# Low parts of the convolution module's weights made ahead and read back from DRAM, early products three pairs in turn, and one sum moved to the norms' PSUM banks, in a two-layer hybrid decoder trunk

## The chip, the cores and the metric

The kernel runs on one core of one Trainium2 chip. The metric is the device time of one execution in microseconds; several executions are timed and the median is given. One further execution was recorded by the hardware profiler, and the views below come from that one.

The engines are named as in the profile: PE is TensorE (matmuls), PEld its weight loads, DVE is VectorE, ACT is ScalarE, POOL is GpSimd, and SP is SyncE, which in this kernel issues every DMA from one in-order queue. L189 is line 189 of the kernel before.

## The reference

The sequence has 1024 positions of width 1024, everything in float32, and two layers. With `rms` for the RMS norm, the reference computes

```python
# layer 0
x = x + fox_attention(rms(x), ...)          # 16 heads, causal, with forget gates
u = rms(x) @ w_up[0]                        # (1024, 1024) @ (1024, 5632)
gate, val = split(causal_dwconv(u, 3 taps) + b, 2)
x = x + (silu(gate) * val) @ w_down[0]      # (1024, 2816) @ (2816, 1024)
# layer 1: the Conformer convolution module
a, g = split(rms(x) @ w_pw1 + b_pw1, 2)     # (1024, 1024) @ (1024, 2048)
u = causal_dwconv(a * sigmoid(g), 31 taps) + b_dw
x = x + silu(rms(u)) @ w_pw2 + b_pw2
# and a feed-forward block as in layer 0, with the weights of layer 1
```

## The kernel before, in words

**Split products.** TensorE reads operands in the type `float32r`. Each float32 operand is split into a high part, a cast (`hi`, on ACT, L183), and a low part, `raw - hi` (`lo`, on POOL or, with `vector=True`, on DVE, L184). `mm3` (L186) then issues three matmuls: high by high, high by low, low by high. So every 128x512 block of a weight costs one DMA, one ACT cast, one subtraction and twelve matmuls (or its share of them). The tiles rotate in rings: eight of `raw`, nine of `whi`, nine of `wlo`.

**Stages.** After the attention and its output projection come, for each layer, the up-projection, the down-projection, and, between the two feed-forward blocks, the convolution module. The sequence is worked in two halves of 512 positions. `trunk` (L973) writes the order of the work out by hand with Python generators: a generator yields after about one block of matmuls, `steps(gen, n)` advances one generator by n yields, and `turns(a, b, n, m)` alternates between two. From L1085 on PE's order is exactly the program's (`manual_schedule`). The order on the other engines and on SP's queue is laid out by the framework when the program is built, and on the chip each engine and SP's queue works strictly in that order.

**Up-projection.** The two halves of the sequence and the two halves of the width make a 2x2 block product that is computed with seven products in place of eight (`combine`, L243, makes the combined factors of the activations; `up`, L306, takes the 22 pairs of gate and value columns). A pair f needs four weight blocks and four sums of them on POOL (L334). Its seven products are called p1 to p7, twelve matmuls each, and their PSUM results are `x` (c11), `y` (c21), `z` (c12) and the sum `w` (c22), each a bank of the pool `pup`, which has six. PE's order within `up` is p1, p6, p2, p5 of pair f, then p4 and p3 of pair f-1, then p7 of pair f.

**Early products.** p1 and p2 need only the first half of the sequence, so `early` (L284) computes them ahead for some pairs, while the second half's norm and the factors are still being made. p1 goes to a PSUM bank and is copied by ACT (L294) to SBUF and from there to DRAM (`p1d`); p2 is then accumulated on the same bank, so its first matmul waits for that copy. The sum goes to DRAM too (`c11d`). In `up` such a pair (f < done) reads both back (L325, L326) and has five products in place of seven. Layer 0 has 12 such pairs, all made just ahead of `up`; layer 1 has all 22, made partly as filler inside the convolution module.

**Down-projection.** `down` (L221) accumulates four banks over 22 blocks of the gated activations, twelve matmuls a step. Per step it splits one block of activations (on DVE) and one of weights (on POOL). The first half of the sequence runs alone (L1109). The second half (`down1`) runs in turns with the convolution module's first half.

**Convolution module.** `conv` (L832) runs once per half. `glu` multiplies with `w_pw1` (48 matmuls for each of the eight column blocks, four weight blocks split on ACT and POOL). `taps_of` applies the 31 taps: 21 on DVE (L885), the other ten as ACT products (L889) summed by POOL (L890). The squares of all column blocks are summed by POOL (L899), and PE reads that sum (L916) before the norm. `rest` multiplies with `w_pw2`. The second half's filler is the first half's `rest` and then `early` of layer 1 (L1122).

**Norms and lag.** A norm block ends in eight PE transposes into the pool `pst` (two banks, also used by the DVE taps' accumulator). With `lag=True` they are put off by `LAG = 3` ticks; a tick is one yield of any generator, whether it held matmuls or not.

Of the kernel before, what the change touches and what calls it, by code (L numbers as in the profile page):

```python
# [16 lines left out]
P = 128  # L17
D = 1024
# [36 lines left out]
LAG = 3  # L55
LEAD = 11
# [12 lines left out]
class Trunk:  # L69
    def __init__(self, ctx, tc):  # L70
        self.tc = tc
        self.nc = tc.nc
        self.ctx = ctx
        self.cp = ctx.enter_context(tc.tile_pool(name="consts", bufs=1, reuse_waits="tile"))
        self.hp = ctx.enter_context(tc.tile_pool(name="ht", bufs=8, reuse_waits="tile"))
        self.mhalf = self.cp.tile([P, 32], F32, name="mhalf")
        self.ident = self.cp.tile([P, P], F32, name="ident")
        make_identity(self.nc, self.ident)
        self.nc.gpsimd.memset(self.mhalf, -0.5)
        self.uid = 0  # L80
        self.lagging = []

# [33 lines left out]
    def norm_block(self, scr, psum, tag, xt, out, tb, stag="scr", lag=False):  # L116
# [16 lines left out]
        if lag:  # L133
            self.lagging.append([LAG, lambda: [turn(q) for q in range(KT // 4)]])
        else:
            for q in range(KT // 4):
                turn(q)

    def tick(self):

        for w in self.lagging:
            w[0] -= 1
        if self.lagging and self.lagging[0][0] <= 0:
            self.lagging.pop(0)[1]()

    def flush(self):
        while self.lagging:
            self.lagging.pop(0)[1]()
# [37 lines left out]
    def mm3(self, out, lh, ll, rh, rl, start, stop, more=False):  # L186

        nc = self.nc
        nc.tensor.matmul(out, lh, rh, start=start, stop=False, skip_group_check=more)  # L189
        nc.tensor.matmul(out, lh, rl, start=False, stop=False, skip_group_check=more)  # L190
        nc.tensor.matmul(out, ll, rh, start=False, stop=stop, skip_group_check=more)  # L191

# [25 lines left out]
    def weight(self, src, shape):  # L218
        return self.halves(self.load(src, shape), shape)

    def down(self, xs, h, nh, lhs, rows, after=None):  # L221
# [4 lines left out]
        for j, (get, r) in enumerate(zip(lhs, rows)):  # L226
            hi, lo = get()
            wh, wl = self.weight(r[:, m], [P, 512])
# [55 lines left out]
    def early(self, l, ht0, w_up, p1d, c11d, count, half):  # L284
# [4 lines left out]
        for f in range(NF):  # L289
            a11, a12 = (self.load(wu[:, 4 * j : 4 * j + 4, f * P : (f + 1) * P], [P, 4, P]) for j in range(2))  # L290
            x = self.bank("e11")
            self.product(x, a11, b11h, b11l, True)
            t = self.ev("p1")
            nc.scalar.copy(t, x)  # L294
            nc.sync.dma_start(p1d[f], t)
            half[0] = True
            yield
            self.product(x, a12, b21h, b21l, False)
            t = self.ev("c11")
            nc.scalar.copy(t, x)  # L300
            nc.sync.dma_start(c11d[f], t)
            count[0] += 1
            half[0] = False
            yield

    def up(self, l, fac, w_up, tab, actd, done, p1d, c11d):  # L306
# [7 lines left out]
        def pair(f):  # L314
# [97 lines left out]
        for f in range(NF):  # L412
# [3 lines left out]
            before = c  # L416
            yield
# [3 lines left out]
    def down_acts(self, xs, l, h, actd, w_down, after):  # L421


        def get(f):
            return lambda: self.halves(self.load(actd[f][:, h * 512 : (h + 1) * 512], [P, 512]), [P, 512], True)

        rows = [w_down[l, f * P : (f + 1) * P, :] for f in range(NF)]
        for nh in range(2):
            yield from self.down(xs, h, nh, [get(f) for f in range(NF)], rows, after if nh == 1 else None)
# [402 lines left out]
    def conv(self, xs, xd, h, ht, w_pw1, taps, vec, w_pw2, halo, after, n_pool=N_POOL):  # L832
# [140 lines left out]
def trunk(ctx, tc, a):  # L973
# [69 lines left out]
    def begin(l, keep):  # L1043
        keep.update(
            done=[0], half=[False], p1d=[dram.tile([P, 512], F32, name=f"p1d{l}_{f}") for f in range(NF)],
# [3 lines left out]
    def early(l, keep):  # L1049
        yield from T.early(l, keep["ht0"], w_up, keep["p1d"], keep["c11d"], keep["done"], keep["half"])  # L1050
# [17 lines left out]
    def ffn_down(l, h, xd, after):  # L1068
        T.fetch_x(xs, xd, h)
        yield from T.down_acts(xs, l, h, actd, a["ffn_w_down"], after)  # L1070
# [14 lines left out]
    ctx.enter_context(tc.manual_schedule(engines={mybir.EngineType.PE}))  # L1085
    begin(0, keep)
# [3 lines left out]
    with ExitStack() as st:  # L1090
# [14 lines left out]
        def conv(h):  # L1105
            return T.conv(xs, xds[1], h, hc[h], a["conv_w_pw1"][0], taps, vec, a["conv_w_pw2"][0], halo,
# [3 lines left out]
        down1 = ffn_down(0, 1, xds[0], conv_norm)  # L1110
        steps(down1, LAG + 3)
        T.flush()
# [5 lines left out]
        steps(rest0, LAG + 4)  # L1118
        T.flush()
        main1, norm1, rest1 = conv(1)  # L1120

        def fill():  # L1122
            yield from rest0
            for _ in range(LAG + 1):
                yield
            T.flush()
# [35 lines left out]
```

## Time and profile before

| | |
|---|---|
| times of three runs | 2494.03, 2494.45 (median), 2496.71 us |
| the profiled execution's own time | 2495.49 us |
| its span, first to last instruction | 2493.6 us |
| PE busy | 2294.3 us (92%), 11282 matmuls |
| DVE, ACT, POOL busy | 1590.4, 1368.6, 1531.9 us |
| moved by DMA | 328.39 MB, mean 132 GB/s |

The profiled execution lies 1.04 us above the median, and its span 1.9 us below its own time. A busy PE is not PE at its peak: a 128x512 matmul is recorded with about 0.39 us, but the next one starts 0.23 us later, so back-to-back matmuls overlap in the records. What a stage of matmuls needs is read from the distance of their starts.

### The profile page before, as it was taken

Reading aid. Unit: us, or ns where it says so; the run is one execution under the profiler, and the core shown is the slowest. Engines: PE = TensorE matmul, PEld = TensorE weight load, DVE = VectorE, ACT = ScalarE, POOL = GpSimd, SP = SyncE. Lnnn points to the kernel's source line nnn. Section 1 sums busy time; section 2 is a strip of 40 time slices with the busy share of each in tenths; the row PEclk is TensorE's granted clock in tenths of the full one; section 3 lists DMA queues with packets and bytes.
Section 4 is the critical chain, followed back from the end, with each engine's and each line's share of the span. In section 5 each row is a group of like instructions: output and inputs, shape, how many; then the busy total and the mean of one; then the engine's idle time right before and its main releaser. Section 6 shows DMA issues by size and latency. Waiting matters only on the chain.

```text
span 2493.6 us, 34983 instructions
## 1 busy us (share of the span) xinstructions
PE 2294.3 (92%) x11282; PEld 1941.0 (78%) x11282; DVE 1590.4 (64%) x2769; ACT 1368.6 (55%) x2919; POOL 1531.9 (61%) x1322
## 2 busy tenths in 40 slices
PE   6899999999879999999999867969798999999999
PEld 6899999987757778888878756847576877778887
DVE  6577777774544675556569975878254676675554
ACT  6566666673444555555456555566453555554443
POOL 2354455451247877763479896879446878864443
PEclk9999999999989999999999988979899999999999
DMA  4222222342343442226554442325244444456664
GB/s 128 61 77 77 77 75 76 106 167 85 118 157 122 143 141 85 89 83 243 194 169 140 135 157 97 95 83 173 94 152 138 137 135 140 136 187 219 200 223 154
DMA packets 320856, 328.39 MB, mean 132 GB/s; under 512 B 22520, under 2 KB 227104, under 8 KB 320672
## 3 DMA queue, kind: packets, MB, share of 16 engines
q1 hardware_dynamic: 320672, 326.16, 40.9%
q8 instruction: 89, 1.46, 0.2%
q14 instruction: 95, 0.78, 0.1%
HBM read 253.13 MB, written 64.55 MB: 127 GB/s over the span
## 4 chain that ended last, share of the span: by engine, by line
PE 47%; POOL 8%; DVE 6%; issue 3%; ACT 3%; DMA 3%; SPq 0%; ACTq 0%; POOLq 0%; DVEq 0%
PE dn L189 7%; PE dn L190 7%; PE dn L191 7%; PE c L189 6%; PE c L190 6%; PE c L191 6%; POOL wlo L184 3%; POOL pacc L890 3%; DMA c<-c11d 2%; PE pw L189 2%; DVE acc L352 2%; PE pw L190 2%; PE pw L191 2%; PE e L189 2%; PE e L190 2%
## 5 line engine op out<-in xcount | busy, mean ns | idle before, releaser
L184 POOL TENSOR_TENSOR wlo<-raw,whi 128x512 fp32r<-128x512 f32 (+1 forms) x432 | 588.6, 1365 | 378.4 <-ACT whi L183 359.0
L183 ACT CAST whi<-raw 128x512 fp32r<-128x512 f32 (+2 forms) x612 | 367.7, 628 | 385.8 <-PE dn L190 212.4
L352 DVE SCALAR_TENSOR_TENSOR acc<-c,ffntab,acc 128x511 f32<-128x511 f32 (+1 forms) x352 | 266.9, 772 | 164.4 <-ACT acc L342 92.4
L189 PE MATMUL c<-bhi,whi 128*128 128x512 f32 x880 | 347.7, 395 | 22.8 <-DVE acc L352 19.2
L184 DVE TENSOR_TENSOR wlo<-raw,whi 128x512 fp32r<-128x512 f32 (+1 forms) x180 | 240.1, 1334 | 163.7 <-ACT whi L183 163.6
L191 PE MATMUL c<-bhi,wlo 128*128 128x512 f32 x880 | 342.9, 390 | 0.0
L190 PE MATMUL c<-blo,whi 128*128 128x512 f32 x880 | 342.8, 390 | 0.0
L184 POOL TENSOR_TENSOR wlo<-sum,whi 128x512 fp32r<-128x512 f32 x176 | 238.7, 1363 | 125.8 <-ACT whi L183 118.7
L189 PE MATMUL dn<-whi,whi 128*128 128x512 f32 x704 | 277.0, 394 | 7.2 <-DVE x L235 6.5
L191 PE MATMUL dn<-whi,wlo 128*128 128x512 f32 x704 | 275.4, 391 | 0.0
L190 PE MATMUL dn<-wlo,whi 128*128 128x512 f32 x704 | 275.4, 391 | 0.0
L885 DVE SCALAR_TENSOR_TENSOR cacc<-u,ctaps,cacc 128x512 f32<-128x512 f32 x320 | 237.1, 752 | 7.4
L189 PEld LDWEIGHTS c<-bhi,whi 128*128 128x128 f32 x880 | 165.1, 188 | 77.7 <-ACT acc L350 36.8
L342 ACT ACTIVATE acc<-c,ffntab 128x512 f32<-128x512 f32 x176 | 136.0, 788 | 132.6 <-DMA c<-c11d 124.1
L890 POOL TENSOR_TENSOR pacc<-pacc,prod 128x512 f32<-128x512 f32 x144 | 196.8, 1366 | 15.1 <-ACT prod L889 10.8
L191 PEld LDWEIGHTS c<-bhi,wlo 128*128 128x128 f32 x880 | 165.2, 188 | 35.2
L190 PEld LDWEIGHTS c<-blo,whi 128*128 128x128 f32 x880 | 165.3, 188 | 32.4
L189 PE MATMUL pj<-whi,hthi 128*128 128x384 f32 (+1 forms) x512 | 179.7, 352 | 6.7 <-ACT sqr L555 3.6
L113 POOL TENSOR_SCALAR ss<-ss 128x4 f32<-128x4 f32 (+1 forms) x96 | 22.5, 234 | 261.6 <-DVE ss L557 116.7
L190 PE MATMUL pj<-wlo,hthi 128*128 128x384 f32 (+1 forms) x512 | 177.4, 346 | 0.6 <-DVE wlo L184 0.6
L191 PE MATMUL pj<-whi,htlo 128*128 128x384 f32 (+1 forms) x512 | 177.8, 348 | 0.0
L643 POOL TENSOR_SCALAR x<-x,nm 128x896 f32<-128x896 f32 (+7 forms) x128 | 100.9, 793 | 104.6 <-DVE nm L642 72.5
(201 smaller groups left out, 5505.3 us busy)
## 6 DMA issues: line engine op xcount, KB each, us to landing
raw<-in_ffn_w_up_dram SPq DMA_DIRECT2D x244, 256.0 KB
raw<-actd SPq DMA_DIRECT2D x176, 256.0 KB
raw<-in_ffn_w_down_dram SPq DMA_DIRECT2D x176, 256.0 KB
raw<-in_conv_w_pw_dram SPq DMA_DIRECT2D x96, 256.0 KB
actd<-acc SPq DMA_DIRECT2D x88, 256.0 KB
raw<-in_fox_w_in_dram SPq DMA_DIRECT2D x64, 192.0 KB
xd<-x SPq DMA_DIRECT2D x24, 512.0 KB
x<-xd SPq DMA_DIRECT2D x24, 512.0 KB
```

Source lines behind the costliest of these rows:

```text
L113: nc.gpsimd.tensor_scalar(ss, ss, 1.0 / n, EPS, op0=ALU.mult, op1=ALU.add)
L183: self.nc.scalar.copy(hi, raw)
L184: (self.nc.vector if vector else self.nc.gpsimd).tensor_tensor(lo, raw, f32(hi), op=ALU.subtract)
L189: nc.tensor.matmul(out, lh, rh, start=start, stop=False, skip_group_check=more)
L190: nc.tensor.matmul(out, lh, rl, start=False, stop=False, skip_group_check=more)
L191: nc.tensor.matmul(out, ll, rh, start=False, stop=stop, skip_group_check=more)
L342: nc.scalar.activation(acc, ps, AF.Identity, bias=tap[3], scale=tap[2])
L352: nc.vector.scalar_tensor_tensor(acc[:, j:], ps[:, : 512 - j], tap[2 - j], acc[:, j:], op0=ALU.mult, op1=ALU.add)
L643: nc.gpsimd.tensor_scalar(X[:, :L], X[:, :L], nm[:, 2:3], 1.0, op0=ALU.mult, op1=ALU.mult)
L885: nc.vector.scalar_tensor_tensor(acc, win(j), tap(j), acc, op0=ALU.mult, op1=ALU.add)
L890: nc.gpsimd.tensor_tensor(pacc, pacc, t, op=ALU.add)
```

## The change

- **Early products three pairs in turn.** `early` runs p1 of three pairs before p2 of the first; from then on p1 and p2 alternate, two pairs apart. When `ffn_up` has used up the lead it sets `stop`, and `early` only finishes the open pairs. The lead in layer 0 falls from 11 to 8 pairs (`LEAD = (8, 11)`).
- **Low parts kept in DRAM.** During layer 0's `up`, 32 blocks of `w_pw1` and 44 of layer 0's `w_down` are loaded, cast on ACT, subtracted on DVE, and their low parts stored to DRAM (`split_ahead`): two after each pair with early products, four after each other pair, the rest after the last. Both halves of the convolution module and the second half of layer 0's down-projection (`down1`) then cast the high part on ACT as before and load the low part with a DMA. In `down1` the activations' low parts move from DVE to POOL (`los is None` becomes False).
- **One sum in the norms' banks.** `w` (c22) takes a bank of `pst` in place of one of `pup`.
- **Lag counted in matmuls.** The lagging transposes come 36 matmuls after their norm block, with at least 12 matmuls between blocks, in place of three ticks. Loops that ran a fixed number of steps now run until nothing is lagging.

The core of the diff:

```diff
-LAG = 3
-LEAD = 11
+LAG = 36
+LEAD = (8, 11)
...
         if lag:
-            self.lagging.append([LAG, lambda: [turn(q) for q in range(KT // 4)]])
+            due = max([self.count + LAG] + [d + 12 for d, _ in self.lagging])
+            self.lagging.append((due, lambda: [turn(q) for q in range(KT // 4)]))
...
         nc.tensor.matmul(out, ll, rh, start=False, stop=stop, skip_group_check=more)
+        self.count += 3
...
-    def weight(self, src, shape):
-        return self.halves(self.load(src, shape), shape)
+    def weight(self, src, shape, lo=None):
+        raw = self.load(src, shape)
+        if lo is None:
+            return self.halves(raw, shape)
+        hi = self.wp.tile(shape, F32R, tag="whi", name=self.n("whi"), bufs=SPLIT_BUFS)
+        low = self.wp.tile(shape, F32R, tag="wlo", name=self.n("wlo"), bufs=SPLIT_BUFS)
+        self.nc.scalar.copy(hi, raw)
+        self.nc.sync.dma_start(f32(low), lo)
+        return hi, low
+
+    def split_ahead(self, src, lo):
+        nc = self.nc
+        shape = list(lo.shape)
+        raw = self.wp.tile(shape, F32R, tag="raw", name=self.n("araw"), bufs=RAW_BUFS)
+        hi = self.wp.tile(shape, F32R, tag="whi", name=self.n("ahi"), bufs=SPLIT_BUFS)
+        nc.sync.dma_start(f32(raw), src)
+        nc.scalar.copy(hi, f32(raw))
+        nc.vector.tensor_tensor(raw, f32(raw), f32(hi), op=ALU.subtract)
+        nc.sync.dma_start(lo, f32(raw))
...
+        open_, f = [], 0
+        while open_ or (f < NF and not stop):
+            if f < NF and not stop:
...
+                x = self.bank("e11")
+                self.product(x, a11, b11h, b11l, True)
...
+                open_.append((f, x, a12))
+                f += 1
+                yield
+            if len(open_) > 2 or stop or f == NF:
+                g, x, a12 = open_.pop(0)
+                self.product(x, a12, b21h, b21l, False)
...
+                done.append(g)
+                yield
...
-                u3, w = half("u3"), self.bank("c22")
+                u3, w = half("u3"), self.pst.tile([P, 512], F32, tag="t", name=self.n("c22"))
...
             before = c
+            for _ in range(min(ahead[f >= done], len(self.ahead))):
+                self.ahead.pop(0)()
             yield
...
         def get(f):
-            return lambda: self.halves(self.load(actd[f][:, h * 512 : (h + 1) * 512], [P, 512]), [P, 512], True)
+            return lambda: self.halves(
+                self.load(actd[f][:, h * 512 : (h + 1) * 512], [P, 512]), [P, 512], los is None
+            )
...
-                    hi, lo = self.weight(wv[:, 4 * q : 4 * q + 4, c0 : c0 + P], [P, 4, P])
+                    hi, lo = self.weight(wv[:, 4 * q : 4 * q + 4, c0 : c0 + P], [P, 4, P], los[2 * ct + s][q])
...
-            lead = 2 * LEAD
-            if T.lagging:
-                steps(first, LAG + 3)
-                lead -= LAG + 3
-            T.flush()
+            lead = 2 * LEAD[l]
+            while T.lagging:
+                steps(first, 1)
+                lead -= 1
...
-            while keep["half"][0]:
-                steps(first, 1)
-            steps(T.up(l, fac, w_up, tabs[l], actd, keep["done"][0], keep["p1d"], keep["c11d"]))
+            keep["stop"].append(True)
+            steps(first)
+            steps(T.up(l, fac, w_up, tabs[l], actd, len(keep["done"]), keep["p1d"], keep["c11d"], (2, 4)))
+            while T.ahead:
+                T.ahead.pop(0)()
...
-        down1 = ffn_down(0, 1, xds[0], conv_norm)
-        steps(down1, LAG + 3)
-        T.flush()
+        down1 = ffn_down(0, 1, xds[0], conv_norm, dnlo)
+        while T.lagging:
+            steps(down1, 1)
...
         def fill():
             yield from rest0
-            for _ in range(LAG + 1):
+            while T.lagging:
                 yield
-            T.flush()
             yield from early(1, keep1)
```

More of the change, by code (lines that the diff above doesn't have):

```diff
@@ L80, in __init__ @@
         self.uid = 0
+        self.count = 0
         self.lagging = []
+        self.ahead = []
     def n(self, s):
@@ L139, in tick @@
     def tick(self):
[L141 to L147, printed above, removed]
+        if self.lagging and self.lagging[0][0] <= self.count:
             self.lagging.pop(0)[1]()
@@ L282, in bank, with early @@
         return self.pup.tile([P, 512], F32, tag="up", name=self.n(m))
-    def early(self, l, ht0, w_up, p1d, c11d, count, half):
+    def early(self, l, ht0, w_up, p1d, c11d, done, stop):
         nc = self.nc
@@ L288, in early, with up @@
         (b11h, b21h), (b11l, b21l) = (m.q for m in ht0)
[L289 to L306, printed above, removed]
+        open_, f = [], 0
+        while open_ or (f < NF and not stop):
+            if f < NF and not stop:
+                a11, a12 = (self.load(wu[:, 4 * j : 4 * j + 4, f * P : (f + 1) * P], [P, 4, P]) for j in range(2))
+                x = self.bank("e11")
+                self.product(x, a11, b11h, b11l, True)
+                t = self.ev("p1")
+                nc.scalar.copy(t, x)
+                nc.sync.dma_start(p1d[f], t)
+                open_.append((f, x, a12))
[4 more added lines that the diff above has]
+                self.product(x, a12, b21h, b21l, False)
+                t = self.ev("c11")
+                nc.scalar.copy(t, x)
+                nc.sync.dma_start(c11d[g], t)
+                done.append(g)
+                yield
+    def up(self, l, fac, w_up, tab, actd, done, p1d, c11d, ahead):
         nc = self.nc
@@ L419, in up, with down_acts @@
             step()
-    def down_acts(self, xs, l, h, actd, w_down, after):
+    def down_acts(self, xs, l, h, actd, w_down, after, los=None):
         def get(f):
-            return lambda: self.halves(self.load(actd[f][:, h * 512 : (h + 1) * 512], [P, 512]), [P, 512], True)
+            return lambda: self.halves(
+                self.load(actd[f][:, h * 512 : (h + 1) * 512], [P, 512]), [P, 512], los is None
+            )
         rows = [w_down[l, f * P : (f + 1) * P, :] for f in range(NF)]
         for nh in range(2):
-            yield from self.down(xs, h, nh, [get(f) for f in range(NF)], rows, after if nh == 1 else None)
+            yield from self.down(
+                xs, h, nh, [get(f) for f in range(NF)], rows, after if nh == 1 else None, los
+            )
     def attn(self, wst0, x_in, gain, w_in, b_f, q_g, k_g, extra=lambda *a: None, early=lambda: None):
@@ L830, in conv_tables, with conv @@
         return taps, vec
-    def conv(self, xs, xd, h, ht, w_pw1, taps, vec, w_pw2, halo, after, n_pool=N_POOL):
+    def conv(self, xs, xd, h, ht, w_pw1, los, taps, vec, w_pw2, halo, after, n_pool=N_POOL):
         nc = self.nc
@@ L1044, in begin @@
         keep.update(
-            done=[0], half=[False], p1d=[dram.tile([P, 512], F32, name=f"p1d{l}_{f}") for f in range(NF)],
+            done=[], stop=[], p1d=[dram.tile([P, 512], F32, name=f"p1d{l}_{f}") for f in range(NF)],
             c11d=[dram.tile([P, 512], F32, name=f"c11d{l}_{f}") for f in range(NF)],
@@ L1049, in early @@
     def early(l, keep):
-        yield from T.early(l, keep["ht0"], w_up, keep["p1d"], keep["c11d"], keep["done"], keep["half"])
+        yield from T.early(l, keep["ht0"], w_up, keep["p1d"], keep["c11d"], keep["done"], keep["stop"])
     def ffn_up(l, keep, first):
@@ L1123, in fill @@
             yield from rest0
-            for _ in range(LAG + 1):
+            while T.lagging:
                 yield
-            T.flush()
             yield from early(1, keep1)
```

25 lines of the change are left out of this document (19 added, 6 removed).

## The prediction, on record before the result was known

> **What bounds the kernel now.** The page first: PE is busy nearly all the time.
>
> ```profile
> span 2493.6 us, 34983 instructions
> PE 2294.3 (92%) x11282; PEld 1941.0 (78%) x11282; DVE 1590.4 (64%) x2769; ACT 1368.6 (55%) x2919; POOL 1531.9 (61%) x1322
> ```
>
> That does not say how much PE could give up, since its records overlap. PE's rows in order of time give the distance of starts:
>
> ```profile
> 1474.30 0.39 PE L191 MATMUL dn<-whi,wlo 128*128 128x512 f32 x1
> 1474.52 0.39 PE L189 MATMUL dn<-whi,whi 128*128 128x512 f32 x1
> 1474.75 0.39 PE L190 MATMUL dn<-wlo,whi 128*128 128x512 f32 x1
> 1474.98 0.39 PE L191 MATMUL dn<-whi,wlo 128*128 128x512 f32 x1
> 1503.70 1.01 PE L916 MATMUL ssps<-ones,sqa 128*128 128x1 f32 x4 [28.34 <-POOL sqa L899]
> ```
>
> Three distances take 0.68 us, so a matmul needs 0.227, a block of twelve 2.72 us. The last row shows what there is to win: PE idle for 28.34 us. So I cut the time from 668 us on into stages, by the tiles that PE works on, and asked the windows view for each (length, then each engine's busy time with its instruction count, granted clock, DMA share, GB/s):
>
> ```profile
> 668.00:773.00 105.00, 77.93 (x298) 59.52 (x297) 50.74 (x54) 46.93 (x88) 61.73 (x45) 0.90 0.51 160
> 773.00:1139.80 366.80, 358.54 (x1563) 291.52 (x1562) 226.01 (x323) 207.66 (x436) 269.14 (x203) 1.00 0.37 119
> 1139.80:1259.80 120.00, 120.00 (x531) 99.34 (x531) 68.20 (x58) 54.20 (x100) 55.68 (x44) 1.00 0.62 206
> 1259.80:1286.00 26.20, 21.89 (x104) 17.68 (x103) 19.01 (x40) 18.11 (x50) 24.99 (x20) 0.93 0.59 193
> 1286.00:1519.20 233.20, 197.66 (x851) 161.63 (x851) 187.51 (x242) 130.78 (x228) 203.27 (x153) 0.92 0.42 132
> 1519.20:1553.20 34.00, 27.10 (x118) 20.93 (x117) 24.59 (x49) 23.18 (x60) 27.51 (x22) 0.90 0.38 132
> 1553.20:1759.30 206.10, 164.74 (x705) 132.81 (x704) 150.81 (x228) 120.26 (x215) 175.81 (x144) 0.91 0.36 114
> 1759.30:1786.70 27.40, 23.29 (x82) 18.27 (x83) 11.89 (x21) 15.04 (x28) 7.67 (x8) 0.82 0.26 87
> 1786.70:1850.80 64.10, 63.80 (x297) 52.67 (x295) 15.29 (x29) 25.66 (x52) 32.09 (x30) 1.00 0.47 148
> 1850.80:1922.90 72.10, 55.63 (x207) 42.38 (x206) 42.98 (x48) 32.10 (x60) 40.80 (x28) 0.91 0.41 131
> 1922.90:2248.00 325.10, 309.41 (x1320) 244.18 (x1319) 222.73 (x322) 187.77 (x406) 247.69 (x183) 1.00 0.46 149
> ```
>
> Length less PE's count times 0.227 is what a stage loses. 32 norm transposes cost 3.9 us (1786.7: 64.1 less 265 x 0.227). The losses: A, early products of layer 0 (668), 105 - 66.8 = 38. B, its `up` (773), 366.8 - 354.8 = 12. The first half's down-projection (1139.8), none. D, lagging norms (1259.8), 26.2 - 20.2 = 6. E, first half of the convolution module in turns with `down1` (1286), 233.2 - 193 = 40. F, norms again (1519.2), 34 - 23.4 = 10.6. G, second half of the module (1553.2), 206.1 - 161.9 = 44 (696 matmuls by the program; some records are missing). H (1759.3), 27.4 - 18.3 = 9. J, early products beside `combine` in layer 1 (1850.8), 72.1 - 47.0 = 25. K, `up` of layer 1 (1922.9), 325.1 - 299.6 = 25.5. Together 210 us. The waits view, for PE, says for whom:
>
> ```profile
> PE e L189 <- ACT p L294: 48.9, 27, 5.9
> PE ssps L916 <- POOL sqa L899: 39.8, 2, 28.3
> PE c L189 <- DVE acc L352: 19.2, 22, 0.9
> PE nps L130 <- DVE y L893: 16.4, 2, 14.0
> PE nps L130 <- DVE htlo L161: 11.8, 11, 3.0
> ```
>
> The first is A, H and J: p2 waits for ACT's copy of p1. The second is the end of E and of G: POOL is late with the taps. The third is K and the end of B, a bank of `pup`. The last two are G's norms.
>
> **Part 1, three pairs in turn (A, H, J).** p2 now comes two blocks, 5.4 us, after its p1; the longest of the 27 waits is 5.9, so nearly all 48.9 us go. What is late next is ACT's own order, where copies stand behind `combine`'s casts. A also shrinks by three pairs: 18 blocks (9 pairs), 49 us, with transposes 1, the 3 us before the first product and a rest of 6 (bounds 2 and 20) make 59 for 105: **-46**. H: 9 to 4, **-5**. J: 25 to 7 (bounds 3 and 15), **-18**. Should layer 1 have a pair less ready, it costs 84 x 0.227 = 19.1 in `up` for the 15.03 derived below and saves 5.4 here: about nothing. Up to three open banks of six are new; when `rest` of the second half starts with two held, its fifth bank must wait for one eviction, about 1 us, inside these rests.
>
> **Part 2, `up` of layer 0 (B).** Three pairs come back with two products each: 72 x 0.227 = 16.3, so PE needs 371.1. Is the wait for a bank what paces the pairs with early products? In layer 1 the chain of waits runs through no matmul for several pairs:
>
> ```profile
> 2044.62 2.55 POOL wlo L184 x2
> ...
> 2047.24 1.63 POOL sum L334
> ...
> 2048.89 0.37 SPq L208
> ...
> 2049.35 3.39 DMA c<-c11d
> ...
> 2052.82 0.83 ACT acc L342
> ...
> 2053.67 1.63 DVE acc L352 x2
> ...
> 2055.92 0.61 ACT whi L183
> ...
> 2056.60 1.72 POOL wlo L184
> ...
> 2059.65 2.55 POOL wlo L184 x2
> ```
>
> One turn takes 2059.65 - 2044.62 = 15.03 us, against 60 x 0.227 = 13.62 on PE. The read of `c11d` stands in SP's queue behind a weight load, which waits for POOL's sums to free its `raw` slot. ACT, DVE and then POOL wait for `c11d`. No bank is in this ring, and PE's wait for one is its consequence: DVE frees the bank late because it was held up. So I cost **one sum in the norms' banks at nothing**: -25.5 in K would be the other end. With 22 turns at 15.03 K would take 330.7; it took 325.1, a head start of 5.6. B's nine pairs lose 9 x 1.41 - 5.6 = 7.
>
> The 76 blocks split ahead are the cost. Two windows inside E price them and all else that follows, the first with DVE subtracting beside POOL, the second with DVE idle; a third row is a DVE subtraction in B:
>
> ```profile
> L890 POOL TENSOR_TENSOR pacc<-pacc,prod 128x512 f32<-128x512 f32 x7 | 12.1, 1727 | 0.0
> L885 DVE SCALAR_TENSOR_TENSOR cacc<-u,ctaps,cacc 128x512 f32<-128x512 f32 x14 | 10.5, 751 | 0.3
> L184 DVE TENSOR_TENSOR wlo<-raw,whi 128x512 fp32r<-128x512 f32 x7 | 9.1, 1301 | 0.0
> L184 POOL TENSOR_TENSOR wlo<-raw,whi 128x512 fp32r<-128x512 f32 x7 | 9.0, 1287 | 0.0
> L183 ACT CAST whi<-raw 128x512 fp32r<-128x512 f32 x14 | 7.9, 610 | 0.0
> ```
> ```profile
> L890 POOL TENSOR_TENSOR pacc<-pacc,prod 128x512 f32<-128x512 f32 x9 | 11.4, 1266 | 0.7
> ```
> ```profile
> L184 DVE TENSOR_TENSOR wlo<-raw,whi 128x512 fp32r<-128x512 f32 x4 | 2.7, 684 | 2.4 <-ACT whi L183 2.4
> ```
>
> One split is 0.61 on ACT, 1.30 on DVE, and 0.46 of hindrance to POOL: 2.35 us if all of it lay in a ring, nothing if all lies in idle time. B leaves DVE 141 us idle and ACT 159; 70 splits need 91 and 43. I take 0.2 us each, 14, nearer to nothing because the idle time is there (bounds 0 and 70 x 2.35 = 164). The splits' loads and stores also pass through SP's queue; a store waits there for DVE, and weight loads wait behind it. B becomes 371 + 7 + 14 = 392, **+25**. The last six splits stand on DVE and ACT before the down-projection's own: **+2** (0 to 8).
>
> **Part 3, the convolution module (E, G).** In E a column block is 96 matmuls, 21.8 us of PE, with four steps of `down1`. POOL: 9 x 1.73 + 1.27 + 8 x 1.29 = 27.2 us. DVE: 21 x 0.751 + two others of 0.7 + 4 x 1.30 = 22.4. Both over PE: POOL falls 5.4 behind per block, and at the end PE waits 28.34. After: `w_pw1`'s four subtractions are gone; of a step's two, one went into the stored low parts and the other moved from DVE to POOL. POOL: 9 x 1.27 + 1.27 + 4 x 1.29 = 17.9; DVE 17.2; both under PE. Then PE is the bound, with some waits left for evictions and the last taps: 40 to 6 (bounds 2 and 20), **-34**. The cover for the 66 low loads is DMA: E moves 132 GB/s x 233.2 = 30.8 MB, plus 66 x 0.262 = 17.3, in 199 us: 242 GB/s. The down-projection runs at 206 with PE never idle; the 36 more are not shown.
>
> G has no `down1`; POOL loses 32 subtractions, 41 us of 176. DVE needs 8 x 17.2 and the norms, about 155, PE 162: nearly even, so I leave 20 of the 44 lost (bounds 12 and 38), **-24**. Six of the 20 are new: the lag now counts matmuls, the filler waits meanwhile, and 72 matmuls of `w_pw1` come no faster than the taps release them.
>
> **Part 4, lag (D, F).** The first transposes come after 36 matmuls, not 24: 2.7 us later, so as much less waiting in each, and a little more in F from a freer DVE: **-7** (0 to -12).
>
> The sum: -46 - 5 - 18 + 25 + 2 - 34 - 24 - 7 = -107. The profiled execution took 2495.49, 1.04 over the median: 2388.5, or **2388** by the median's measure.
>
> **The rivals.**
>
> *The bank does free `up`.* If the ring of 15.03 was only laid out so because of the bank, K and B fall towards POOL's nine operations, 9 x 1.29 = 11.6, and PE binds: -20 and -7, 2361. Against it: the first pairs of K ran on PE's pace while the ring already turned at its own.
>
> *The splits sit in the ring.* DVE and POOL shut each other out for a whole instruction: DVE 0.68 + 1.29 = 1.97, POOL 0.68 more, ACT 0.61, 3.26 per split. Pairs with early products: 15.03 + 2 x 3.26 - 13.62 = 7.9 over PE, nine times 71. The other 13: a ring without the 3.39 of `c11d` but with two more subtractions, 14.2, plus 4 x 3.26 = 27.2, 8.2 over 19.1: 106. In all 177 for the 21 above: 2544, **slower**. It cancels the gain from 2.6 us per split. For it: 1727 against 1266 on POOL and 1301 against 684 on DVE. Against: the measured mixture gives 2.35, and idle time takes some. The Trainium skill, "SBUF — State Buffer", section "Who interferes with whom", speaks for this rival: a DVE instruction with two SBUF inputs contends with a GpSimd instruction that reads SBUF, and the loser is held for the whole instruction. The trace agrees in part, 1727 beside such subtractions, and 1287 where DVE ran the taps, which have one SBUF input.
>
> *The low parts come late.* A low load must wait in SP's in-order queue for its `wlo` slot and holds the loads behind it. If half a landing (3.39 / 2) shows on PE for one in three of 98 loads, 55 us, E and G gain almost nothing: 2443. For it, SP's queue already blocks in `up`; against it, nine slots are four steps, 10.9 us, ahead of PE.
>
> **How the numbers follow.** Forecast 0.67, the bank 0.13, late low parts 0.12, splits in the ring 0.08. The range reaches from the bank's case with the terms at their better ends (2361 - 20) to late low parts: 2340 to 2446. About 0.2% is what a measurement of this kernel can tell. Faster 0.90, the same 0.02, slower 0.08.
>
> **What would show it.** Part 1: the wait for L294 falls from 48.9 to under 10, and A lasts about 59. Part 2: B lasts about 390 with reads of `c11d` still 15 us apart in K, PE's waits there moved from a bank to subtractions. Part 3: the wait for POOL's sum of squares falls from 39.8 to under 10, additions of `pacc` to 1.27. Wrong would be: B over 420, a DMA among PE's waits in E, or K under 310.

## The result and the profile after

The kernel after takes **2429.47 us** (median of four runs, 2421.41 to 2430.27) against 2495.58 (2494.03 to 2496.78) for the kernel before on the same chip: a ratio of 0.9728, 95% interval 0.9706 to 0.9750. That is 66 us saved where the prediction said 107. The time lies inside the range, 41 us above the forecast, and that distance is the sum of misses of both signs.

The profiled execution took 2430.27 us by its own time. From the page of the kernel after, the span and the engines:

```profile
span 2428.5 us, 35460 instructions
PE 2281.0 (94%) x11282; PEld 1948.8 (80%) x11282; DVE 1654.8 (68%) x2801; ACT 1410.9 (58%) x2992; POOL 1480.1 (61%) x1258
```

DVE has 64 us more, POOL 52 us less. The stages, cut at the same matmuls as before, in the windows view of the kernel after (columns as in the prediction). In this order they are A, B, C with D, E, G, the stretch from the second half's `rest` to the end of J, and K:

```profile
672.00:747.00 75.00, 57.85 (x227) 45.31 (x226) 60.14 (x56) 40.90 (x79) 52.09 (x35) 0.89 0.59 182
747.00:1158.40 411.40, 380.85 (x1633) 308.83 (x1632) 294.03 (x395) 249.29 (x516) 289.26 (x212) 0.98 0.60 194
1158.40:1301.10 142.70, 140.24 (x634) 115.80 (x632) 79.16 (x85) 72.96 (x148) 79.83 (x62) 1.00 0.75 246
1301.10:1503.50 202.40, 195.33 (x851) 160.99 (x852) 147.14 (x210) 133.40 (x233) 154.60 (x123) 0.98 0.74 236
1532.70:1731.30 198.60, 165.05 (x706) 133.95 (x705) 152.02 (x236) 120.40 (x220) 144.50 (x118) 0.90 0.49 151
1753.20:1878.60 125.40, 116.06 (x513) 94.78 (x512) 62.62 (x80) 60.27 (x118) 80.56 (x57) 0.97 0.49 155
1878.60:2182.30 303.70, 301.09 (x1322) 248.81 (x1321) 257.58 (x322) 193.08 (x406) 270.73 (x187) 0.99 0.52 164
```

Read the second column against the lengths before. B has grown from 366.8 to 411.4, and K has fallen from 325.1 to 303.7 with the same matmuls: there PE now has almost no idle time. The waits view of the kernel after, for PE:

```profile
PE c L186 <- DVE u L410: 26.4, 8, 6.3
PE e L186 <- ACT p L313: 21.4, 6, 6.6
PE nps L132 <- DVE htlo L158: 19.0, 10, 3.9
PE ssps L944 <- POOL sqa L927: 16.0, 2, 9.6
PE nps L132 <- DVE y L921: 10.8, 1, 10.8
```

The wait for a bank of `pup` (19.2 us before, on DVE's taps) is gone. The wait for the copy of p1 is down from 48.9 to 21.4, that for the sum of squares from 39.8 to 16.0. New at the head is a wait of `up` for DVE's u3, the sum of `y` and p1 after p7: p4 accumulates on the bank that u3 reads, and DVE is late.

Twelve variants are told below. Their stages, cut at the same matmuls (us; "after" and "before" for comparison; times are medians, ratios to the kernel before as run on the same chip):

| | time | ratio (95%) | A | B | C, D | E | G | K |
|---|---|---|---|---|---|---|---|---|
| before | 2495.58 | 1 | 105.2 | 366.6 | 146.2 | 233.3 | 206.1 | 325.3 |
| after | 2429.47 | 0.9728 (0.9706–0.9750) | 75.0 | 411.4 | 142.7 | 202.4 | 198.6 | 303.7 |
| no_ahead | 2425.62 | 0.9723 (0.9700–0.9746) | 77.5 | 371.5 | 151.1 | 230.0 | 203.5 | 300.8 |
| ahead_no_sub | 2396.38 | 0.9612 (0.9597–0.9626) | 73.9 | 382.7 | 142.7 | 203.6 | 197.8 | 300.8 |
| ahead_pool | 2413.54 | 0.9681 (0.9665–0.9698) | 78.0 | 395.9 | 147.5 | 202.8 | 198.9 | 300.9 |
| ahead06 | 2441.85 | 0.9791 (0.9775–0.9807) | 77.3 | 422.8 | 142.7 | 203.5 | 197.8 | 304.5 |
| bank_alone | 2456.87 | 0.9857 (0.9826–0.9888) | 105.1 | 355.4 | 145.5 | 228.5 | 205.9 | 301.4 |
| bank_undone | 2457.03 | 0.9847 (0.9824–0.9870) | 76.1 | 415.8 | 146.7 | 202.2 | 197.8 | 325.3 |
| taps_later | 2493.32 | 1.0002 (0.9989–1.0016) | 104.4 | 362.8 | 145.4 | 234.2 | 206.3 | 324.6 |
| turn_undone | 2445.50 | 0.9799 (0.9775–0.9823) | 80.7 | 399.5 | 142.7 | 203.6 | 199.2 | 306.7 |
| norm_bank | 2412.99 | 0.9677 (0.9663–0.9691) | 76.1 | 406.8 | 142.9 | 203.5 | 191.6 | 300.9 |
| best0 | 2425.31 | 0.9734 (0.9712–0.9756) | 78.1 | 371.5 | 149.8 | 235.1 | 198.6 | 300.8 |
| best52 | 2400.40 | 0.9634 (0.9611–0.9658) | 77.3 | 384.8 | 142.7 | 211.3 | 189.6 | 301.3 |
| best32 | 2398.17 | 0.9633 (0.9606–0.9659) | 77.7 | 377.6 | 144.3 | 213.4 | 191.6 | 300.9 |

The code ahead of A was not edited in any of them, yet its length lies between 666.6 and 672.7 us: differences of some 5 us between two times mean nothing by themselves. The stages are from one profiled execution each, and K, whose program lines are the same, came out between 300.8 and 306.7 in the runs that keep the bank's edit: a stage difference of some 5 us is no more than a hint either.

### The profile page after: what moved, and what is told of

Same layout as the page of the kernel before. It is cut to its first block, busy times and chain, and to the rows that moved or that the text cites. A ratio compares the mean times of both kernels' runs of the same rounds, so it can differ in the third digit from the quotient of the medians.

```text
span 2428.5 us, 35460 instructions
## 1 busy us (share of the span) xinstructions
PE 2281.0 (94%) x11282; PEld 1948.8 (80%) x11282; DVE 1654.8 (68%) x2801; ACT 1410.9 (58%) x2992; POOL 1480.1 (61%) x1258
## 5 line engine op out<-in xcount | busy, mean ns | idle before, releaser
L181 POOL TENSOR_TENSOR wlo<-raw,whi 128x512 fp32r<-128x512 f32 (+1 forms) x368 | 522.1, 1422 | 373.5 <-ACT whi L180 361.7
L180 ACT CAST whi<-raw 128x512 fp32r<-128x512 f32 (+2 forms) x504 | 306.0, 632 | 298.1 <-PE dn L187 191.9
L374 DVE SCALAR_TENSOR_TENSOR acc<-c,ffntab,acc 128x511 f32<-128x511 f32 (+1 forms) x352 | 280.4, 805 | 89.1 <-ACT edge L367 61.4
L181 DVE TENSOR_TENSOR wlo<-raw,whi 128x512 fp32r<-128x512 f32 (+1 forms) x136 | 182.1, 1342 | 140.1 <-ACT whi L180 139.9
L181 POOL TENSOR_TENSOR wlo<-sum,whi 128x512 fp32r<-128x512 f32 x176 | 250.5, 1430 | 29.1 <-ACT whi L180 23.5
L918 POOL TENSOR_TENSOR pacc<-pacc,prod 128x512 f32<-128x512 f32 x144 | 186.7, 1297 | 22.7 <-ACT prod L917 15.2
L115 POOL TENSOR_SCALAR ss<-ss 128x4 f32<-128x4 f32 (+1 forms) x96 | 21.6, 225 | 272.4 <-ACT hn L123 122.4
```

Source lines behind the costliest of these rows:

```text
L115: nc.gpsimd.tensor_scalar(ss, ss, 1.0 / n, EPS, op0=ALU.mult, op1=ALU.add)
L180: self.nc.scalar.copy(hi, raw)
L181: (self.nc.vector if vector else self.nc.gpsimd).tensor_tensor(lo, raw, f32(hi), op=ALU.subtract)
L374: nc.vector.scalar_tensor_tensor(acc[:, j:], ps[:, : 512 - j], tap[2 - j], acc[:, j:], op0=ALU.mult, op1=ALU.add)
L918: nc.gpsimd.tensor_tensor(pacc, pacc, t, op=ALU.add)
```

## The experiments

My theory after the result: the splits made ahead in B cost about what they save in E, and the bank, which I had priced at nothing, is what frees K. Its rival: the splits are worth their 34 us in E, and B grew for another reason (the banks or the order of the early products).

### The splits: do they pay?

**no_ahead**, the kernel after with every weight split where it is used:

```diff
-                    hi, lo = self.weight(wv[:, 4 * q : 4 * q + 4, c0 : c0 + P], [P, 4, P], los[2 * ct + s][q])
+                    hi, lo = self.weight(wv[:, 4 * q : 4 * q + 4, c0 : c0 + P], [P, 4, P])
...
+    T.ahead.clear()
...
-        down1 = ffn_down(0, 1, xds[0], conv_norm, dnlo)
+        down1 = ffn_down(0, 1, xds[0], conv_norm)
```

> The changed kernel without the blocks split ahead: the convolution module and down1 split their low parts as the kernel before did (weights on POOL, down1's activations on DVE), all else as changed. Theory 1, the splits stand in the ring of layer 0's up-projection and cost about 40 us there, nearly what they save later: layer 0's up-projection 411 to about 372 us, the module's first half 203 to about 230, its second 199 to about 205, the whole within 10 us of 2429. Theory 2, the splits are hidden and the 45 us by which layer 0's up-projection grew come from the three pairs moved into it and from the bank: it stays at 400 or more, and the whole rises by 30 us or more, to about 2460.

Measured: 2425.62 us, no slower than the kernel after. Without splits B takes 371.5 us, which is PE's need of 371.1: so all 40 us over it are the splits'. They give back 27.6 in E, 8.4 in C and D, 4.9 in G: 41. **The largest part of the change, by lines, gives nothing net** that these runs could tell.

What paces the pairs with early products shows in the reads of `c11d`, one per such pair. The tile view, SP's row in layer 0's `up` (first and last start), of the kernel after, then of no_ahead:

```profile
L348 SPq DMA_DIRECT2D c<-c11d x7: 338/456/497, 775.6 to 879.4; - x7
```
```profile
L348 SPq DMA_DIRECT2D c<-c11d x7: 339/456/457, 769.1 to 848.9; - x7
```

Six distances: 17.3 us a pair with two splits in it, 13.3 without. PE itself needs 60 x 0.227 = 13.62 a pair, so not all of the difference reaches it. The windows rows give what does: the first 516 matmuls of B, which are the nine pairs with early products but for p4 and p3 of the last, and the rest; first the kernel after, then no_ahead:

```profile
747.00:891.90 144.90, 123.08 (x517) 98.37 (x516) 102.68 (x129) 78.58 (x163) 105.75 (x76) 0.98 0.56 180
891.90:1158.40 266.50, 257.78 (x1117) 210.46 (x1116) 191.36 (x267) 170.71 (x354) 183.51 (x136) 0.99 0.62 201
```
```profile
748.90:865.90 117.00, 117.00 (x518) 96.89 (x517) 92.56 (x115) 74.03 (x152) 110.30 (x78) 1.00 0.47 144
865.90:1120.40 254.50, 253.22 (x1117) 209.32 (x1116) 146.75 (x209) 143.20 (x295) 173.06 (x134) 1.00 0.31 99
```

The nine pairs lose 27.9 us to 18 splits, 1.55 each. The rest loses 12.0 to the others, 0.2 each, and about half of that is one wait for u3 at its end, 6.3 long where no_ahead has 1.3.

Why two splits cost so much shows in the timeline of the kernel after, in one such pair (rows of PE and others left out):

```profile
802.91 1.74 POOL L356 TENSOR_TENSOR sum<-raw,raw 128x512 f32<-128x512 f32 x1
803.42 1.77 DVE L235 TENSOR_TENSOR araw<-araw,ahi 128x512 fp32r<-128x512 f32 x1
...
805.22 0.32 SPq L236 DMA_DIRECT2D pwlo<-araw  x1
805.23 0.62 ACT L234 CAST ahi<-araw 128x512 fp32r<-128x512 f32 x1 [2.71 <-DVE araw L235]
...
805.75 0.62 ACT L180 CAST whi<-sum 128x512 fp32r<-128x512 f32 x1
...
806.45 2.60 POOL L181 TENSOR_TENSOR wlo<-sum,whi 128x512 fp32r<-128x512 f32 x2 [1.80 <-ACT whi L180]
...
807.95 0.15 ACT L367 COPY edge<-c 128x2 f32<-128x2 f32 x1
...
808.13 1.53 DVE L374 SCALAR_TENSOR_TENSOR acc<-c,ffntab,acc 128x511 f32<-128x511 f32 x2 [0.90 <-ACT edge L367]
...
810.98 0.46 SPq L348 DMA_DIRECT2D c<-c11d  x1
...
811.52 0.68 DVE L410 TENSOR_TENSOR u<-c,p 128x512 f32<-128x512 f32 x1
```

The subtraction runs beside a sum on POOL and takes 1.77 us. Two in-order queues stand still until it ends: on SP the store of its result, with weight loads behind it, and on ACT the second split's cast, idle for 2.71 us, with the casts of two sums behind it. POOL waits 1.80 for the first of those. ACT's copy `edge` stands behind the casts too, and DVE itself waits 0.90 for it, then works without a gap until u3 (811.52). So one step on DVE, which is idle for 28% of B, holds ACT, POOL and the weight loads; u3 comes late, and PE's next row waits for it:

```profile
812.25 0.50 PE L186 MATMUL c<-bhi,whi 128*128 128x512 f32 x1 [3.04 <-DVE u L410]
```

The store costs more than its place in the queue. A split's `araw` takes a slot of the ring of eight `raw`, and the slot is free only when the store from it has landed. The waits view for SP's queue in the kernel after, 747 to 891.9 us, has both waits:

```profile
SPq L206 <- DMA pwlo<-araw: 18.5, 8, 2.8
SPq L236 <- DVE araw L235: 12.1, 8, 4.9
```

L206 is the load of `up`'s weights, L236 the store. POOL's sums of two blocks wait 16.1 us for weight loads in these pairs, and 0.3 in no_ahead.

**ahead_no_sub**: as after, but the split's subtraction on DVE is left out, so the stored blocks are the weights themselves and not low parts.

```diff
-        nc.vector.tensor_tensor(raw, f32(raw), f32(hi), op=ALU.subtract)
```

> The changed kernel whose split ahead leaves out DVE's subtraction, so that the stored blocks are the weights themselves and not their low parts; loads, casts and stores stay. Theory 1, the subtraction beside POOL (DVE's time and the shared port) is the cost of a split: layer 0's up-projection 411 to about 380 us. Theory 2, the cost is the split's load and store in SP's queue and the raw slots it holds: the stage stays above 400.

Measured: B falls by 28.7 of the 40 us, to 382.7, and the whole to 2396.38, as its first theory said. Loads, casts and stores cost 11.2; the subtraction, with all that is held behind it, the rest. The store then waits for its load alone and no longer for ACT and DVE, so the split is loosened in more than DVE's time.

**ahead_pool**: the same subtraction on POOL.

```diff
-        nc.vector.tensor_tensor(raw, f32(raw), f32(hi), op=ALU.subtract)
+        nc.gpsimd.tensor_tensor(raw, f32(raw), f32(hi), op=ALU.subtract)
```

> The changed kernel with the split's subtraction on POOL in place of DVE. Theory 1, what costs is that DVE and POOL hold each other up: on one engine the hindrance goes, pairs with early products fall from 17.2 to about 15.5 us and the whole to about 2415. Theory 2, any work added to the ring costs its own time, and POOL has the least room (12 of 13.7 us): pairs rise to 17.5 or more and the whole to 2435 or more.

Measured: B 395.9, 15.5 better than on DVE, and 15.3 us between the reads of `c11d` (17.3 on DVE), as its first theory said; C and D are 4.8 worse. So POOL is the better place in B, though its operations are what the ring runs through: what the subtraction held up from DVE was dearer than a place in POOL's own order.

**ahead06**: no splits in the pairs with early products, six in each other pair.

```diff
-    steps(T.up(..., keep["c11d"], (2, 4)))
+    steps(T.up(..., keep["c11d"], (0, 6)))
```

> The changed kernel with the splits placed elsewhere: none after the nine pairs with early products, six after each of the other thirteen (2 and 4 before). Theory 1, a split costs where the ring sets the pace (pairs with early products) and is nearly free where PE does (19.1 us of matmuls per pair): the first kind goes from 17.2 back to about 14 us, the other from 19.7 to 20.5 at most, layer 0's up-projection from 411 to about 390 and the whole to about 2408. Theory 2, each split costs its half microsecond wherever it stands: the stage stays at 411 and the whole within 6 us of 2429.

Measured: slower than after, 2441.85 us, B 422.8. The early pairs are free again, but thirteen pairs with six splits cost 51.3 over no_ahead, 3.9 each. Both theories miss: the first said 390 and 2408, the second a stage that stays at 411. So no single price per split holds: a pair without early products takes some for little (best52 below: four for 1.0 on average), and six cost nearly four times that. From 900 us to the end of B, POOL's sums of two blocks wait 54.7 us for weight loads; in best52 it is 12.0.

### The bank

**bank_alone**, the kernel before with the bank's edit and no other:

```diff
-                u3, w = half("u3"), self.bank("c22")
+                u3, w = half("u3"), self.pst.tile([P, 512], F32, tag="t", name=self.n("c22"))
```

> The kernel before with only the sum w in a bank of pst. Theory 1 (the bank set the pace): layer 1's up-projection 325 to about 304 us and layer 0's down by some 7, the whole about 2467. Theory 2 (the ring holds no bank, as predicted): layer 1's pairs stay at 15.0 us, the whole within 5 us of 2495.

and **bank_undone**, the kernel after with `w` back in `pup` (the same two lines, reversed):

> The changed kernel with the sum w back in a bank of pup. Theory 1, the bank set the pace of layer 1's up-projection after all: its pairs go from 13.7 back to 15.0 us, the stage from 304 to 325, the whole to about 2450. Theory 2, the ring (POOL, SP's queue, c11d, ACT, DVE) was broken by something else, the order of SP's queue with early products in turn: pairs stay near 13.7 and the whole within 5 us of 2429.

Measured: alone the edit takes 24 us from K and 11 from B, 1.4% of the whole; undone, it gives the 21.6 of K back. One line, priced at nothing, is about half of what the change gains (39 us alone, 28 undone, of 66). The reads of `c11d` in layer 1's `up`, before and in bank_alone:

```profile
L326 SPq DMA_DIRECT2D c<-c11d x19: 339/457/459, 1943.4 to 2215.4; - x19
```
```profile
L326 SPq DMA_DIRECT2D c<-c11d x19: 378/457/1286, 1925.5 to 2173.2; - x19
```

Eighteen distances: 15.1 us before, 13.8 in bank_alone, PE's own need being 13.62. The ring no longer turns slower than PE. Which step went out of it shows in ACT's rows of the timeline. First before, in the turn that the prediction shows as a chain:

```profile
2052.82 0.82 ACT L342 ACTIVATE acc<-c,ffntab 128x512 f32<-128x512 f32 x1 [4.53 <-DMA c<-c11d]
...
2055.38 0.63 ACT L356 ACTIVATE acc<-acc 128x512 f32<-128x512 f32 x1 [1.67 <-DVE acc L352]
2055.92 0.60 ACT L183 CAST whi<-sum 128x512 fp32r<-128x512 f32 x1
```

and in bank_alone:

```profile
2024.57 0.82 ACT L342 ACTIVATE acc<-c,ffntab 128x512 f32<-128x512 f32 x1 [1.36 <-DMA c<-c11d]
...
2025.37 0.62 ACT L183 CAST whi<-sum 128x512 fp32r<-128x512 f32 x1
2028.02 0.63 ACT L356 ACTIVATE acc<-acc 128x512 f32<-128x512 f32 x1 [2.03 <-DVE acc L352]
```

Before, the cast that POOL waits for comes 3.10 us after the taps' first step (2055.92 - 2052.82), behind the silu that waits for DVE. In bank_alone it stands ahead of that silu, at 0.80 us. 2.3 us less in a ring of 15.1 would make 12.8 by this estimate, below PE's 13.62. POOL's waits for ACT's casts in K fall from 71.9 us to 21.8. The program's lines there are the same; the order on ACT is laid out by the framework, and it came out otherwise when the bank's pool changed. It went back with the bank: in bank_undone the silu stands ahead of the cast again in all 19 turns, and the reads are 15.1 us apart, while the kernel after has bank_alone's order and 13.8. The reads in K, bank_undone, then the kernel after:

```profile
L348 SPq DMA_DIRECT2D c<-c11d x19: 382/456/1701, 1904.3 to 2176.2; - x19
```
```profile
L348 SPq DMA_DIRECT2D c<-c11d x18: 338/456/1328, 1912.5 to 2147.1; - x18
```

**taps_later** was to tell the order from the bank: the kernel before, bank untouched, with the c11 taps written later, so that ACT's order changes.

```diff
-                return [loads, lambda: taps(0, 0, st["x"]), p6, p5], [p7], [p4, p3]
+                return [loads, p6, p5, lambda: taps(0, 0, st["x"])], [p7], [p4, p3]
```

> The kernel before, with c22 still in a bank of pup; in `up` the ACT and DVE taps of c11 are only written after p6 and p5 for pairs with early products, which changes the order laid out on ACT. If what the bank did in layer 1's `up` came by way of ACT's order (a cast of a sum ahead of the silu that waits for the late c11d), layer 1's `up` falls from 325 to about 302 us with no bank moved, layer 0's by some 5 to 10, and the whole to about 2465 (2455 to 2475). If the bank itself was what was missing, the stage stays at 325, reads of c11d stay 15 us apart, and the whole stays at 2493 (2488 to 2498).

Measured: 2493.32 us, no change, with the reads in K 15.1 us apart:

```profile
L326 SPq DMA_DIRECT2D c<-c11d x19: 338/457/1854, 1942.3 to 2213.4; - x19
```

By its number this is the bank's side. But the trace shows that in K the cast still follows the silu as before, so the order under test was not made, and the run doesn't tell. That the bank's edit frees K is shown both ways; that it does so by ACT's order is argued. It stays open whether the other order alone, with `w` in `pup`, would do it. What speaks for the order is that the chain of the slow turn holds no matmul and no wait for a bank.

### Three pairs in turn

**turn_undone**, the kernel after with p2 right behind its p1:

```diff
-            if len(open_) > 2 or stop or f == NF:
+            if len(open_) > 0 or stop or f == NF:
```

> The changed kernel with p2 of a pair right after its p1 again (8 pairs in layer 0 in place of 9). Theory 1, three in turn hid the wait for ACT's copy: that wait comes back from 21 to about 45 us and the whole goes to about 2455. Theory 2, what remains of the wait is ACT's own lateness behind combine, and the turn only moved it: the whole within 8 us of 2429.

Measured: 2445.50, 16 us slower than after. PE's wait for ACT's copy comes back from 21.4 to 56.1 us, more than its first theory said, and the whole rises by less (2455 was expected). Its J stretch takes 139.4 (125.4 after) and H 27.7 (21.9). A is 5.7 longer with one pair less in it, and B is 11.9 shorter, with one pair less that carries two splits.

What keeps A at 75 shows in the waits view of the kernel after, for PE in A:

```profile
PE e L186 <- ACT p L313: 13.1, 4, 6.6
```

and for ACT, which makes those copies:

```profile
ACT bhi L271 <- DVE t L279: 11.4, 4, 5.5
ACT bhi L271 <- DVE t L280: 4.8, 3, 2.4
```

ACT waits for DVE's sums in `combine`, and the copies of p1 stand behind those casts. So p2 still waits for the copy of its own p1, only less often. And a long wait of PE cost more here than its length. In A, after the longest (PE's rows):

```profile
722.99 0.80 PE L186 MATMUL e<-hthi,whi 128*128 128x512 f32 x1 [6.60 <-ACT p L313]
723.58 0.63 PE L187 MATMUL e<-htlo,whi 128*128 128x512 f32 x1
724.01 0.63 PE L188 MATMUL e<-hthi,wlo 128*128 128x512 f32 x1
724.44 0.63 PE L186 MATMUL e<-hthi,whi 128*128 128x512 f32 x1
```

After it a dozen matmuls start 0.43 us apart, not 0.227; the clock granted in A is 0.89 on the mean. Added up over A, starts that lie 0.26 to 0.5 us apart cost 5.4 us, beside 16.5 of longer gaps.

### The norms' banks, and better versions

The waits of G in the kernel after hold `PE nps L132 <- DVE y L921`, 10.8 us: transposes of the lagging norms need a bank of `pst` that the DVE taps hold. **norm_bank** puts these norms (the ones ahead of layer 1's feed-forward block) into `pup`:

```diff
-            T.norm_block(T.scr, pst, "t", xs[tb], out, tb, lag=lag)
+            T.norm_block(T.scr, *((T.pup, "up") if lag else (pst, "t")), xs[tb], out, tb, lag=lag)
```

> The changed kernel with the lagging norm transposes before layer 1's feed-forward block in banks of pup in place of pst, which the taps' accumulators also use. Theory 1, the second half of the convolution module loses its time because a transpose waits for an accumulator's bank: PE's wait of 10.8 us for the taps' sum goes, the stage from 199 to about 186, the whole to about 2418. Theory 2, DVE is late in any case and only the name of the wait changes: the whole within 4 us of 2429.

Measured: 2412.99, 16 us better than after (13 by the two ratios), of which G gives 7.0 (191.6) where its first theory said 13. The profiled executions differ by 17: most of the rest lies ahead of A (3.2), in B (4.6) and in K (2.8), where no line of the edit stands, and no run explains it. The wait for `y` is gone, but the end of G now waits longer for the taps' sum of squares. PE's waits in G, norm_bank:

```profile
PE ssps L944 <- POOL sqa L927: 24.9, 1, 24.9
PE e L187 <- DVE htlo L158: 2.8, 1, 2.8
```

So G's limit is the taps, and PE's earlier waits were partly spent on time that the taps need anyway.

The last three runs put this together with fewer splits. **best0** is no_ahead with norm_bank's edit:

> The kernel after without any split ahead, and with the lagging norms ahead of layer 1's feed-forward block transposing into pup's banks. If the 7 us that the other banks gave in the second half of the convolution module are independent of the splits: about 2416 (2407 to 2422). If they were only there because low parts come from DRAM: 2426, as without splits.

Measured: 2425.31, the same as no_ahead, as the second reading said. G gains 4.9 and E loses 5.1, so in the whole the norms' edit gained nothing without the stored low parts; why E is longer no run shows.

**best52** splits 52 blocks ahead (the 32 of `w_pw1` and 20 of `w_down`), four after each pair without early products and none after the others; **best32** only the 32 of `w_pw1`, three after each such pair, `(0, 3)`. The other blocks are split where they are used, and the activations beside them on DVE. The edit beside best0's norms, for best52:

```diff
-    steps(T.up(..., keep["c11d"], (2, 4)))
+    steps(T.up(..., keep["c11d"], (0, 4)))
```

> As the run before it in this call, but with 52 blocks split ahead, four after each pair of layer 0's `up` that has no early products and none after the others: all 32 of w_pw1 and the first 20 of down1's first half; the rest is split as in the kernel before. If the splits cost 3.5 us per pair with early products and 0.65 per other pair, layer 0's `up` takes about 380 us (371 without splits, 411 with all), the first half of the convolution module about 212, and the whole 2392 (2382 to 2404). If the cost goes with the number of splits, wherever they stand, `up` takes 371 + 52/76 x 40 = 398 and the whole about 2410.

> As the run before it in this call, with only the 32 blocks of w_pw1 split ahead, three after each pair of layer 0's `up` without early products; down1 is as in the kernel before. By the first reading `up` takes about 376, the first half of the module 214 to 222 and the whole 2394 (2385 to 2408); by the cost per split, 371 + 32/76 x 40 = 388 and about 2408.

Measured: 2400.40 and 2398.17, which can't be told apart; both ranges held. By the ratios both are about 1% below the kernel after. In best32, B takes 377.6, 6.1 over no_ahead: 0.19 us a split. In best52 it is 13.3, or 0.26. On the mean that is the 0.2 us that the prediction took, but it is no price that each split pays. PE runs through most of these pairs at its own pace, and most of the loss lies in one wait, in best32 the first of these rows and in best52 the second, in its last pair:

```profile
1064.76 0.79 PE L186 MATMUL c<-hthi,whi 128*128 128x512 f32 x1 [4.37 <-ACT p L390]
```
```profile
1127.29 0.76 PE L186 MATMUL c<-bhi,whi 128*128 128x512 f32 x1 [9.14 <-DVE u L410]
```

The windows row of best32 for B:

```profile
747.40:1125.00 377.60, 371.94 (x1633) 307.20 (x1632) 265.10 (x355) 232.83 (x477) 288.34 (x211) 1.00 0.49 155
```

For the same PE count as after's, 33.8 us less; DVE's busy time is 265 in place of 294. best32, with fewer blocks stored, is the version to keep.

## Why the prediction was right and wrong, step by step

Forecast against measured, by stages (us of the profiled executions): A -46, came -30.2. H -5, -5.4. J -18, -10.8. B +25, +44.8. C, D and F, with the last splits, -5, -8.2. E -34, -30.9. G -24, -7.5. K 0, -21.6. Ahead of A and at the end 0, +4.7. The sums are -107 and -65.1. Two slips of the working are small: 0.61 + 1.30 + 0.46 is 2.37, not 2.35, and 107 below the median of 2494.45 is 2387, not 2388.

- **Part 3, E: right.** E lost 9.4 us after (202.4 - 193) where 6 was forecast, and of the 30.9 gained no_ahead shows 27.6 to be the stored low parts'. Moving the subtractions lets POOL keep up, additions of `pacc` take 1.30 us in place of the mixture of 1.73 and 1.27, and no DMA is among PE's waits in E, so the low parts do not come late. The sign "under 10" for the wait for the sum of squares was missed: it is 16.0, of which 6.4 in E. From the page of the kernel after:

```profile
L918 POOL TENSOR_TENSOR pacc<-pacc,prod 128x512 f32<-128x512 f32 x144 | 186.7, 1297 | 22.7 <-ACT prod L917 15.2
```

- **Part 2, the splits: the term that was mis-sized.** "I take 0.2 us each, 14, nearer to nothing because the idle time is there" measured 40, 0.53 each: inside its bounds, but nearly three times the term. The idle time is there; the step that failed is the inference from an engine's idle share to the price of an instruction in in-order queues. In the nine pairs with early products, where a ring already stood near PE's pace, a split costs PE 27.9 / 18 = 1.55 us, in the others 0.2 on the mean. In the nine the rival *the splits sit in the ring* had the place right and the size too large (71 us for 27.9), but not in the thirteen others, where it priced 106 and 12.0 came; hence its 2544 did not come. The 7 us that the prediction left to the ring of these pairs itself did not come either: no_ahead, which keeps the bank's edit, is at 371.5 for PE's 371.1.
- **Part 2, the bank: wrong.** "One sum in the norms' banks at nothing", since "no bank is in this ring". The ring was read rightly: no matmul is in it. What failed is the step from there to nothing: the edit took the ring from 15.1 to 13.8 us all the same. It silently took the order on ACT to stay when a tile changes its pool, and that order changed; whether it is the whole cause stays open. The upper end, -25.5 in K, was near the truth (-21.6), and "K under 310", which the prediction named as what would prove it wrong, came. The rival *the bank does free up* had the gains about right (-20 and -7, and -23.9 and -11.2 came in bank_alone), with 0.13.
- **Part 1: right in kind, too large.** turn_undone is 16 us slower. But p2 still waits for its own p1's copy: 21.4 us in 6 waits where "under 10" was the sign, and 13.1 of them in A. The "rest of 6 (bounds 2 and 20)" in A came out at 22 (75 - 53), over its bound: "what is late next is ACT's own order" was named and priced too low, and 5.4 of it are slow starts after waits, which have no term in the sum. J's rest came out at 14 (125.4 - 64.1 - 47.0), just under its bound of 15.
- **Part 3, G: mis-sized.** "I leave 20 of the 44 lost (bounds 12 and 38)" measured 36.6 (198.6 - 162), just inside them. PE, DVE and POOL being nearly even in sum did not make them even in order; waits for the taps' bank, their sum and the norms' low parts came one after the other.
- **Part 4: the number right, the way not shown.** C, D and F gave -8.2 with the tail's splits for -5. But no_ahead keeps the lag's edit, and there C and D are 4.9 longer than before, and F 5.3 shorter: with D as it is there, the lag gives next to nothing, and D's gain comes with the stored low parts. No run undoes the lag alone.

A, J, B and G together fell 59 us short of the forecast, and K gave back 22 that it had not asked for. Without these 22 the time would have been about 2451, above the range's end of 2446: that it lies inside is luck in part.

## What to carry to other kernels

The idle share of an engine does not price a new instruction: ask which in-order queues stand behind it, and whether a ring there already turns near the pace of the bound; in this kernel the same split cost PE 0.2 us on the mean beside slack, 1.55 in the ring, and 0.66 where six came in one pair. Where a framework lays out the order of the engines, an edit that moves no work can still move the order (here one changed with the bank, both ways), so a part priced at nothing deserves a run by itself. And where a change is a pair of cost and gain in different stages, undo it alone before believing the sum.

## What the runs showed of the hardware

Of DVE's 76 subtractions made ahead, most ran unhindered: 18 took over 1 us, the slowest two and a half times the median. The tile view of the kernel after (shortest, median and longest, ns):

```profile
L235 DVE TENSOR_TENSOR araw<-araw,ahi x76: 673/692/1783, 739.0 to 1143.6; 128x512 fp32r<-128x512 f32 x76
```

In the turn shown above, the subtraction (803.42 to 805.19) ends 0.54 us after the sum on POOL beside it (802.91 to 804.65), and it takes 1.77 where the median is 0.69. The Trainium skill, "SBUF — State Buffer", section "Who interferes with whom", says that a DVE instruction with two SBUF inputs contends with a GpSimd one that reads SBUF, and it calls the shared ports an exclusive lock. By that the subtraction, which came second, would end 0.69 us after POOL's sum; at 0.54 the trace agrees nearly. The hold itself (1.1 us, in five of the nine pairs with early products) is the smaller part of what these pairs lost, 3.1 each. In twelve of the thirteen others one subtraction is held as long, and the thirteen lost 12.0 us in all. What made the difference, as the rows above read, is what ACT and SP had queued behind it.
